# Holding the issue order of three engines in the last down units of a macaron decoder trunk, and handing finished tiles of x on one per product

## The chip, the cores and the metric

The kernel runs on one core of a Trainium2 chip. The metric is device time in microseconds (us). The engines are named as the profile names them: PE (TensorE, matmuls), DVE (VectorE), ACT (ScalarE), POOL (GpSimd) and SP (SyncE, which here only issues DMAs). Each engine runs its own list of instructions in order and waits for the others by semaphores.

## The reference

Two layers of a decoder work on x, 512 tokens by 1024 channels. Each layer is a half-weighted feed-forward block, a mixer, and another half-weighted feed-forward block, all with an RMS norm in front:

```python
def swiglu(x, w_gate, w_up, w_down):
    return (jax.nn.silu(x @ w_gate) * (x @ w_up)) @ w_down

for layer in range(DEPTH):                  # DEPTH = 2, D_MODEL = 1024, D_FF = 2816
    x = x + 0.5 * swiglu(rms_norm(x, ffn1_norm[layer]), ...)
    hn = rms_norm(x, mix_norm[layer])
    x = x + (pool_mla_mixer(hn, ...) if layer % 2 == 0 else gated_conv_mixer(hn, ...))
    x = x + 0.5 * swiglu(rms_norm(x, ffn2_norm[layer]), ...)
```

So there are four feed-forward blocks: the first ends into the attention mixer, the second into the third, the third into the convolution mixer, and the fourth into the stores of the output.

## The kernel before

x lies transposed in SBUF as eight tiles `x[0]` to `x[7]` of 128 channels by 512 tokens. All matrix products are done in split precision: each operand is a high part (`hi`, fp32r) and a low part (`lo`, the rest), and `mm3` or `product` (L489) issues three matmuls for each block, `hi*hi`, `hi*lo`, `lo*hi`. Weights come from memory in fp32. The function `split` makes the two parts: ACT casts (`whi`, L87), then DVE subtracts (`wlo`, L88). Three pairs of `whi`/`wlo` buffers go round, so a split can start only when the product three places earlier has left its buffer.

A feed-forward block is cut into units: `gate_up` units, one for each pair of hidden blocks, and `down` units, which add two by two tiles into x. Each unit is a block matrix product done in seven smaller products, P1 to P7, instead of eight (Strassen's scheme in Winograd's form). The sums of weight blocks that this needs are made by DMA: after P1, P5 and P6 have split their weight tile (`ar` or `sto`), a POOL-issued DMA adds the next block into the same tile (`Seven.add`, L124), and a later product of the unit (P7, P6, P3) splits that sum. The sums of activation blocks are made on DVE (`blocks`), and `put` splits them into `hh` tiles (L87 and L88 again).

A fixed list, made by `staggered`, says in which order the products of all units come. Its last part, with unit 12 the last `gate_up` and 13 and 14 the last two `down` units, is

```
12.P6 12.P2 12.P7 12.P3 12.P4  13.P1 13.P5 13.P2 13.P6 14.P5 13.P7 14.P1 13.P3 13.P4  14.P6 14.P2 14.P7 14.P3 14.P4
```

This text calls it the tail; there are four of them. A product is named by unit and step. One of unit 12 has 24 matmuls of 128x256, one of units 13 and 14 has 18 (three hidden blocks). `weights()` is called at the start of each product and emits the split for the product two places later. The result of a down product is added into two tiles of x (`add`, L560). Tiles 0 and 1 are final after 13.P3, 2 and 3 after 13.P4, 4 and 5 after 14.P3, 6 and 7 after 14.P4.

A final tile is handed to the next stage by `after(k)`. In the first three blocks that is `norm_in`: ACT squares it (`sq`, L247), POOL adds the square to `acc` (L252, L254), ACT scales it into the high part `xs` (L241) and DVE makes the low part (L242). For `k == 4` it also runs a small square root `d` (L260), which makes ACT load the table for square roots. In the last block `after` is `store`, a DMA to the output. Before the change all four tiles of a down unit are handed on after its P4.

The order on each engine isn't the order of the text: a scheduler places every instruction by its own estimate of when it can run, within the dependencies. Only the program order of what is emitted, plus that estimate, decides what stands ahead of what.

Of the kernel before, what the change touches and what calls it, by code (L numbers as in the profile page):

```python
# [1 line left out]

# [1 line left out]

# [32 lines left out]
GROUPS = ((0, 4), (4, 8), (8, 11))  # L37
# [4 lines left out]
def trunk(ctx: ExitStack, tc: tile.TileContext, a, out):  # L42
# [12 lines left out]
    nc = tc.nc  # L55
# [8 lines left out]
    def bank(tag="bank", bufs=None):  # L64
        return pp.tile([P, 512], F32, tag=tag, name=tag, bufs=bufs)
# [82 lines left out]
    def staggered(kinds, full):  # L148

        order = [(0, "P5"), (0, "P1")]
        for i, kind in enumerate(kinds):
            if i == full + 1:
                order += [(i, s) for s in ("P1", "P5", "P2", "P6")]
                order += [(i + 1, "P5"), (i, "P7"), (i + 1, "P1"), (i, "P3"), (i, "P4")]
            else:
                order += [(i, s) for s in ("P6", "P2", "P7")]
                if i + 1 == len(kinds) or i == full:
                    order += [(i, "P3"), (i, "P4")]  # L160
                else:
                    order += [(i + 1, "P5"), (i, "P3"), (i + 1, "P1"), (i, "P4")]
        return order
# [3 lines left out]
    for l in range(2):  # L167
        for f in ("ffn1", "ffn2"):
# [15 lines left out]
            what = []  # L184
            for gi, (p0, p1) in enumerate(GROUPS):
                last = gi + 1 == len(GROUPS)
# [3 lines left out]
            for kind, p in what:  # L190
                if kind == "gu":
                    units.append(seven([gu[p, q] for q in range(4)], CH, turn))
                else:
                    gi, e = p
                    p0, p1 = GROUPS[gi]
                    n = 2 * (p1 - p0) * P
                    w = a[f"{f}_w_down{gi}"][l]
                    units.append(seven([w[e, q] for q in range(4)], n, turn))
            order = staggered([k for k, _ in what], max(j for j, (k, _) in enumerate(what) if k == "gu"))
# [2 lines left out]
    ready = []  # L202
    loaded = [0]
    used = [0]

    def weights(ahead=3, fetched=6):
        i = used[0]
        used[0] += 1
        while len(ready) < min(i + ahead, len(chunks)):
            while (loaded[0] < min(max(len(ready) + 1, i + fetched), len(chunks))  # L210
                   and chunks[loaded[0]].turn <= now[0]):
                chunks[loaded[0]].load()
                loaded[0] += 1
            ready.append(chunks[len(ready)].halves())
        return ready[i]
# [124 lines left out]
    def ffn(l, f, which, after, first=False):  # L340
        what, order = plans[l, f]
        with ExitStack() as es:
# [139 lines left out]
            def product(ps, e, w, acts, fresh):  # L482
                hi, lo = w
                for k, (ah, al) in enumerate(acts):
                    s = slice((e * len(acts) + k) * P, (e * len(acts) + k + 1) * P)
                    o = ps[:, e * HT:(e + 1) * HT]
                    last = e == 1 and k == len(acts) - 1
                    for i, (w_, a_) in enumerate(((hi, ah), (hi, al), (lo, ah))):
                        nc.tensor.matmul(o, w_[:, s], a_, start=fresh and e == 0 and k == 0 and i == 0,  # L489
                                         stop=last and i == 2, skip_group_check=True)  # L490
# [54 lines left out]
            def down(i, p, s):  # L545
                gi, e0 = p
                p0, p1 = GROUPS[gi]
                u = live.setdefault(i, {})
                if s in ("P1", "P5", "P2"):
                    u[{"P1": "X", "P5": "Y", "P2": "Z"}[s]] = bank()  # L550
                ps = u["Z" if s == "P2" else "Y" if s in ("P5", "P3") else "X"]
                w = weights()
                for e in range(2):
                    product(ps, e, w, [hfac[q][right[s]] for q in range(p0, p1)], s in ("P1", "P5", "P2"))
                o11, o12, o21, o22 = (xt[:, 4 * e0 + 2 * i2:4 * e0 + 2 * i2 + 2, j * HT:(j + 1) * HT]
                                      for i2 in range(2) for j in range(2))
                v = ps.rearrange("p (e t) -> p e t", t=HT)

                def add(o, sign):
                    nc.vector.scalar_tensor_tensor(o, v, 0.5 * sign, o, ALU.mult, ALU.add)  # L560

                add({"P1": o11, "P2": o11, "P6": o12, "P3": o12, "P7": o22, "P5": o22, "P4": o21}[s],
                    -1.0 if s in ("P7", "P3", "P4") else 1.0)
                if gi == len(GROUPS) - 1 and s == "P4":
                    for k in range(4 * e0, 4 * e0 + 4):
                        after(k)

            for n, (i, s) in enumerate(order):
                if n == 3:
                    blocks(1, hz, False)  # L570
                    blocks(1, hz, True)
                kind, p = what[i]
                (gate_up if kind == "gu" else down)(i, p, s)

    def store(m):
        (nc.sync if m % 2 else nc.scalar).dma_start(out=out[m], in_=x[m])
# [371 lines left out]
    def odd_mixer(after):  # L948
        with tc.tile_pool(name="op", bufs=1) as op:
# [31 lines left out]
            for m in range(NK):  # L981
# [3 lines left out]
                after(m)  # L985

    ffn(0, "ffn1", 0, lambda m: norm_in(m, 1), True)
    even_mixer(lambda m: norm_in(m, 2))
    ffn(0, "ffn2", 2, lambda m: norm_in(m, 3))
    ffn(1, "ffn1", 3, lambda m: norm_in(m, 4))  # L990
    odd_mixer(lambda m: norm_in(m, 5))
    ffn(1, "ffn2", 5, store)
# [71 lines left out]
```

## Time and profile before

| what | value |
|---|---|
| median of three runs | 1735.53 us (1734.84 to 1741.09) |
| the profiled execution, its own time | 1735.6 us |
| its span, first to last instruction | 1733.9 us |
| granted clock of PE, mean | 0.996 of full speed |
| PE busy | 1692.3 us, 98% |
| DVE busy | 1312.8 us, 76% |
| ACT busy | 889.7 us, 51% |
| POOL busy | 299.2 us, 17% |

The profile is of one execution. A span runs from the first to the last instruction, and 1.7 us of the execution's own time lie around it. Busy shares are means over all stages. A matmul's end is modelled, so a matmul of 128x256 is drawn 0.28 us long although the next may start 0.11 us after it: an idle time that the profile shows on PE is therefore about 0.16 us shorter than the time in which PE could have started another.

### The profile page before, as it was taken

To read this page: it belongs to the slowest core of one execution; us is meant where nothing else is said; L and a number is where in the kernel's file an instruction comes from. 1 tells how busy PE (TensorE), PEld (TensorE's weight loads), DVE (VectorE), ACT (ScalarE), POOL (GpSimd) and SP (SyncE) were. 2 spreads that over 40 slices of the span, in tenths; PEclk is the share of its full clock that TensorE was granted. 3 is DMA by queue.
4 is the path that set the end of the run, shared out by engine and by line. 5 is a ranking of instruction groups with operands and counts; after the bars stand their busy time and mean duration, and the time that the engine had idled before them with its cause. 6 is when DMAs were issued, how large, how long until landed. Compare 5 with 4: busy or idle time off the path is not lost.

```text
span 1733.9 us, 30670 instructions
## 1 busy us (share of the span) xinstructions
PE 1692.3 (98%) x12354; PEld 1574.8 (91%) x12354; DVE 1312.8 (76%) x1883; ACT 889.7 (51%) x1268; POOL 299.2 (17%) x343
## 2 busy tenths in 40 slices
PE   7999999999999999999999999999999999999998
PEld 5799999977888899999988999998888879999998
DVE  5977786877897977786798867868655678867766
ACT  5554554564665564554565545545322345545553
POOL 2021111234202012111221112112000201121111
PEclk8999999999999999999999999999999999999999
DMA  6489988741015489989756898896322247998985
GB/s 219 108 213 221 220 213 213 160 147 37 19 43 169 119 217 215 217 219 217 158 179 148 218 223 205 212 208 138 112 98 98 97 142 180 211 218 210 216 209 131
DMA packets 86878, 294.76 MB, mean 170 GB/s; under 512 B 10448, under 2 KB 11216, under 8 KB 86736
## 3 DMA queue, kind: packets, MB, share of 16 engines
q0 software_dynamic: 34560, 121.65, 39.9%
q1 hardware_dynamic: 50512, 169.89, 28.0%
q8 instruction: 97, 1.59, 0.4%
q10 hardware_dynamic: 1664, 1.26, 0.2%
q14 instruction: 45, 0.37, 0.1%
HBM read 290.67 MB, written 2.10 MB: 169 GB/s over the span
## 4 chain that ended last, share of the span: by engine, by line
PE 82%; DVE 9%; issue 4%; ACT 2%; DMA 2%; POOL 1%; SPq 0%; ACTq 0%; DVEq 0%; POOLq 0%
PE bank L489 59%; PE bank L220 6%; PE bank L218 6%; PE bank L219 6%; DVE wlo L88 2%; DMA sto<-in_ffn_w_down 1%; ACT whi L87 1%; DVE xn L379 1%; DMA sto<-in_ffn_w_gu 1%; PE bank L895 1%; DVE xs L242 1%; PE held L218 0%; PE held L219 0%; PE held L220 0%; DVE x L560 0%
## 5 line engine op out<-in xcount | busy, mean ns | idle before, releaser
L489 PE MATMUL bank<-hh,whi 128*128 128x256 f32 x2464 | 427.6, 277 | 6.5 <-ACT whi L87 3.6
L489 PEld LDWEIGHTS bank<-hh,whi 128*128 128x128 f32 x2464 | 373.0, 188 | 9.8 <-ACT whi L87 4.6
L489 PE MATMUL bank<-hh,wlo 128*128 128x256 f32 x1232 | 340.5, 277 | 5.4 <-DVE wlo L88 5.4
L87 ACT CAST whi<-sto 128x1024 fp32r<-128x1024 f32 (+1 forms) x180 | 183.5, 1021 | 242.6 <-PE bank L489 140.0
L489 PE MATMUL bank<-fT,whi 128*128 128x256 f32 x1728 | 303.6, 278 | 0.0
L88 DVE TENSOR_TENSOR wlo<-sto,whi 128x1024 fp32r<-128x1024 f32 (+1 forms) x180 | 214.1, 1189 | 97.0 <-ACT whi L87 96.1
L489 PEld LDWEIGHTS bank<-fT,whi 128*128 128x128 f32 x1728 | 262.2, 188 | 2.0 <-ACT x L495 1.5
L489 PE MATMUL bank<-fT,wlo 128*128 128x256 f32 x864 | 239.1, 278 | 0.0
L489 PEld LDWEIGHTS bank<-hh,wlo 128*128 128x128 f32 x1232 | 231.1, 188 | 6.2 <-DVE wlo L88 6.2
L489 PE MATMUL bank<-fN,whi 128*128 128x256 f32 x1152 | 208.3, 283 | 3.5 <-ACT x L495 0.7
L218 PE MATMUL bank<-xs,whi 128*128 128x512 f32 x520 | 206.0, 397 | 2.5 <-DVE t L456 2.0
L220 PE MATMUL bank<-xs,wlo 128*128 128x512 f32 x520 | 204.4, 394 | 3.2 <-DVE wlo L88 3.1
L219 PE MATMUL bank<-xs,whi 128*128 128x512 f32 x520 | 204.9, 394 | 1.8 <-DVE xs L242 1.5
L489 PE MATMUL bank<-fB,whi 128*128 128x256 f32 x1152 | 205.9, 278 | 0.0
L87 ACT CAST whi<-a 128x1024 fp32r<-128x1024 f32 (+1 forms) x120 | 123.0, 1025 | 139.1 <-PE bank L489 88.0
L124 POOL DMA_DIRECT2D sto<-in_ffn_w_gu x108 | 94.4, 874 | 565.6 <-DVE wlo L88 285.3
L489 PEld LDWEIGHTS bank<-fN,whi 128*128 128x128 f32 x1152 | 174.2, 188 | 13.8 <-DVE c L532 8.4
L88 DVE TENSOR_TENSOR wlo<-a,whi 128x1024 fp32r<-128x1024 f32 (+1 forms) x120 | 142.6, 1188 | 53.0 <-ACT whi L87 52.7
L88 DVE TENSOR_TENSOR wlo<-ar,whi 128x1024 fp32r<-128x1024 f32 (+1 forms) x120 | 142.5, 1188 | 49.2 <-ACT whi L87 49.0
L87 ACT CAST whi<-ar 128x1024 fp32r<-128x1024 f32 (+1 forms) x120 | 122.6, 1021 | 106.1 <-PE bank L489 59.2
L489 PEld LDWEIGHTS bank<-fB,whi 128*128 128x128 f32 x1152 | 176.3, 188 | 0.0
L87 ACT CAST whi<-raw 128x1024 fp32r<-128x1024 f32 (+2 forms) x91 | 86.9, 958 | 163.6 <-PE bank L219 143.1
(242 smaller groups left out, 3028.9 us busy)
## 6 DMA issues: line engine op xcount, KB each, us to landing
sto<-in_ffn_w_gu POOLq DMA_DIRECT2D x108, 512.0 KB, 7.5
a<-in_ffn_w_gu SPq DMA_DIRECT2D x72, 512.0 KB, 6.2
sto<-in_ffn_w_down POOLq DMA_DIRECT2D x48, 512.0 KB, 7.7
sto<-in_ffn_w_gu SPq DMA_DIRECT2D x36, 512.0 KB, 4.7
ar<-in_ffn_w_gu SPq DMA_DIRECT2D x36, 512.0 KB, 5.4
ar<-in_ffn_w_gu POOLq DMA_DIRECT2D x36, 512.0 KB, 5.5
a<-in_ffn_w_down SPq DMA_DIRECT2D x32, 512.0 KB, 6.2
raw<-in_ffn_w_gu SPq DMA_DIRECT2D x31, 512.0 KB, 4.6
```

The costliest lines, as they stand in the source:

```text
L87: nc.scalar.copy(hi, raw)
L88: nc.vector.tensor_sub(lo, raw, hi.bitcast(F32))
L124: nc.gpsimd.dma_start(out=self.unit[tag], in_=self.srcs[q], accum_op=ALU.add)
L218: nc.tensor.matmul(ps, wh, ah, start=start, stop=False)
L219: nc.tensor.matmul(ps, wh, al, start=False, stop=False)
L220: nc.tensor.matmul(ps, wl, ah, start=False, stop=stop)
L242: nc.vector.scalar_tensor_tensor(xl, x[k], g, xh.bitcast(F32), ALU.mult, ALU.subtract)
L379: nc.vector.scalar_tensor_tensor(xn[e][:, i], x[k], gains[:, which, k:k + 1], R if e else Rp, ALU.mult, ALU.mult)
L489: nc.tensor.matmul(o, w_[:, s], a_, start=fresh and e == 0 and k == 0 and i == 0, stop=last and i == 2, skip_group_check=True)
L895: nc.tensor.transpose(ps[:, kt * P:(kt + 1) * P], p[:, kt * P:(kt + 1) * P], ident)
```

## The change

From 12.P6 on to the end of each feed-forward block, a context manager gives every instruction of PE, DVE and ACT a dependency, without a semaphore, on the instruction of the same engine that was emitted before it. The scheduler then keeps these three engines in program order there. POOL, SP and the DMAs aren't held. And tiles of x are handed on earlier and singly: 0 and 1 become available at 13.P3, 2 and 3 at 13.P4, and one is handed on at the end of each down product from there on, so tile 0 after 13.P3, 1 after 13.P4, 2 after 14.P6, 3 after 14.P2, none after 14.P7, 4 after 14.P3, 5 after 14.P4, and 6 and 7 right behind.

```diff
+    @contextmanager
+    def in_order():
+
+        traced = nc.cur_bb.bb.instructions
+        n = len(traced)
+        yield
+        before = {}
+        for k, i in enumerate(traced):
+            if i.engine in (nc.tensor.engine, nc.vector.engine, nc.scalar.engine):
+                if k >= n and i.engine in before:
+                    tc.add_manual_dep(i, before[i.engine], mybir.DependencyInfo(
+                        mybir.DependencyClass.NoSync, mybir.DependencyReason.DATA), reason="in_order")
+                before[i.engine] = i.name
...
-                if gi == len(GROUPS) - 1 and s == "P4":
-                    for k in range(4 * e0, 4 * e0 + 4):
-                        after(k)
-
+                if gi == len(GROUPS) - 1 and s in ("P3", "P4"):
+                    k = 4 * e0 + 2 * (s == "P4")
+                    done.extend((k, k + 1))
+                if done:
+                    after(done.pop(0))
+
+            done = []
+            last = order.index((len(what) - 3, "P6"))
+            pin = ExitStack()
             for n, (i, s) in enumerate(order):
+                if n == last:
+                    pin.enter_context(in_order())
                 if n == 3:
                     blocks(1, hz, False)
                     blocks(1, hz, True)
                 kind, p = what[i]
                 (gate_up if kind == "gu" else down)(i, p, s)
+            for k in done:
+                after(k)
+            pin.close()
```

Lines behind the new function stand 14 higher in the changed kernel (L560 becomes L574, L242 becomes L256), and L87 and L88 keep their numbers.

The first place is DVE in the first tail, from the result `c` of 12.P3 on. `hz` are activation blocks that are rebuilt, `hh` their low parts, and `wlo<-sto` is the split for 13.P5, `wlo<-a_3518` that for 13.P2. Before:

```order
L536 SCALAR_TENSOR_TENSOR c<-bank,x_3479 128x512
L88 TENSOR_TENSOR wlo<-sto,whi 128x768
L502 TENSOR_TENSOR hz<-c 128x256
L438 TENSOR_TENSOR hz<-hz 128x256
L440 SCALAR_TENSOR_TENSOR hz<-hz 128x256
L439 TENSOR_TENSOR hz<-hz 128x256
L542 SCALAR_TENSOR_TENSOR hz<-bank,c 128x256
L88 TENSOR_TENSOR hh<-hz,hh 128x512 x2
L88 TENSOR_TENSOR hh<-hz,hh 128x256
L448 SCALAR_TENSOR_TENSOR hz<-hz 128x256
L88 TENSOR_TENSOR wlo<-a_3518,whi 128x768
L88 TENSOR_TENSOR hh<-hz,hh 128x512
```

In the changed kernel the same stretch of DVE reads:

```order
L550 SCALAR_TENSOR_TENSOR c<-bank,x_3479 128x512
L516 TENSOR_TENSOR hz<-c 128x256
L452 TENSOR_TENSOR hz<-hz 128x256
L453 TENSOR_TENSOR hz<-hz 128x256
L454 SCALAR_TENSOR_TENSOR hz<-hz 128x256
L88 TENSOR_TENSOR hh<-hz,hh 128x512 x2
L88 TENSOR_TENSOR hh<-hz,hh 128x256
L88 TENSOR_TENSOR wlo<-sto,whi 128x768
L556 SCALAR_TENSOR_TENSOR hz<-bank,c 128x256
L462 SCALAR_TENSOR_TENSOR hz<-hz 128x256
L88 TENSOR_TENSOR hh<-hz,hh 128x512
L88 TENSOR_TENSOR wlo<-a_3518,whi 128x768
```

The split for 13.P5 moved from the second place to behind the three low parts of the rebuilt blocks, and the split for 13.P2 moved behind the last of them. On ACT the cast for 13.P5 likewise moved from ahead of the three `hh` casts to behind them.

The second place is DVE later in the same tail, from the add of 13.P3 on: `x<-bank` is the add of a down product, `xs` the low part of a tile handed on, and `wlo` the splits for 14.P2, 14.P7, 14.P3 and 14.P4. Before:

```order
L560 SCALAR_TENSOR_TENSOR x<-bank,x 128x2x256
L88 TENSOR_TENSOR wlo<-a_3762,whi 128x768
L242 SCALAR_TENSOR_TENSOR xs_3864<-x,gains,xs_3864 128x512
L560 SCALAR_TENSOR_TENSOR x<-bank,x 128x2x256
L242 SCALAR_TENSOR_TENSOR xs_3864<-x,gains,xs_3864 128x512
L88 TENSOR_TENSOR wlo<-ar,whi 128x768
L560 SCALAR_TENSOR_TENSOR x<-bank,x 128x2x256
L242 SCALAR_TENSOR_TENSOR xs_3875<-x,gains,xs_3875 128x512 x2
L560 SCALAR_TENSOR_TENSOR x<-bank,x 128x2x256
L88 TENSOR_TENSOR wlo<-sto,whi 128x768
L88 TENSOR_TENSOR wlo<-a_3835,whi 128x768
```

In the changed kernel the same stretch reads:

```order
L574 SCALAR_TENSOR_TENSOR x<-bank,x 128x2x256
L256 SCALAR_TENSOR_TENSOR xs_3839<-x,gains,xs_3839 128x512
L88 TENSOR_TENSOR wlo<-a_3762,whi 128x768
L574 SCALAR_TENSOR_TENSOR x<-bank,x 128x2x256
L256 SCALAR_TENSOR_TENSOR xs_3839<-x,gains,xs_3839 128x512
L88 TENSOR_TENSOR wlo<-ar,whi 128x768
L574 SCALAR_TENSOR_TENSOR x<-bank,x 128x2x256
L256 SCALAR_TENSOR_TENSOR xs_3900<-x,gains,xs_3900 128x512
L88 TENSOR_TENSOR wlo<-sto,whi 128x768
L574 SCALAR_TENSOR_TENSOR x<-bank,x 128x2x256
L256 SCALAR_TENSOR_TENSOR xs_3900<-x,gains,xs_3900 128x512
L88 TENSOR_TENSOR wlo<-a_3842,whi 128x768
```

Add, low part and split now follow each other in every product; the two low parts that stood together ahead of the split for 14.P3 (`wlo<-sto`) are parted, and every split stands behind the low part of the product before.

The third place is ACT at the very start of the program, which the change doesn't name: the five small square roots `d` were all placed there before, since they depend on a constant alone. Before:

```order
L260 ACTIVATE d<-eps 128x1 x5
L87 CAST whi<-raw 128x2x256
L241 ACTIVATE xs_122<-x,gains 128x512
L247 ACTIVATE sq<-x 128x512
L241 ACTIVATE xs_122<-x,gains 128x512
L87 CAST whi<-raw 128x2x256
L247 ACTIVATE sq<-x 128x512
L241 ACTIVATE xs_129<-x,gains 128x512 x2
L241 ACTIVATE xs_151<-x,gains 128x512
L247 ACTIVATE sq<-x 128x512 x2
```

In the changed kernel ACT starts with:

```order
L87 CAST whi<-raw 128x2x256
L255 ACTIVATE xs_122<-x,gains 128x512 x2
L87 CAST whi<-raw 128x2x256
L255 ACTIVATE xs_129<-x,gains 128x512 x2
L261 ACTIVATE sq<-x 128x512 x2
L255 ACTIVATE xs_151<-x,gains 128x512
L261 ACTIVATE sq<-x 128x512 x2
L255 ACTIVATE xs_151<-x,gains 128x512
```

The square roots left for the tails, and the first square now comes behind the fourth scaled tile instead of behind the first. Elsewhere, outside the tails and the first matmuls behind them, the lists of DVE and ACT are the same.

## Rows read from the trace of the kernel before

**Rows 1.** The first line of the page: span and instructions.

```profile
span 1733.9 us, 30670 instructions
```

**Rows 2.** Waits of PE: who waited for whom; us in total, times, longest.

```profile
PE held L316 <- DVE acc L322: 6.8, 1, 6.8
PE bank L489 <- DVE wlo L88: 6.3, 6, 1.7
PE bank L489 <- ACT whi L87: 3.6, 5, 0.8
...
PE bank L489 <- DVE hh L88: 1.8, 4, 0.5
...
PE bank L219 <- DVE xs L242: 1.5, 4, 0.6
...
PE bank L489 <- ACT hh L87: 1.0, 4, 0.3
```

**Rows 3.** Timeline of PE, first tail: start, length, [idle before <- releaser].

```profile
319.20 0.50 PE L489 MATMUL bank<-hh,whi 128*128 128x256 f32 x2 [0.85 <-ACT whi L87]
...
353.36 0.38 PE L489 MATMUL bank<-hh,wlo 128*128 128x256 f32 x1 [1.58 <-DVE wlo L88]
353.58 0.40 PE L489 MATMUL bank<-hh,whi 128*128 128x256 f32 x2
...
357.34 0.39 PE L218 MATMUL bank<-xs,whi 128*128 128x512 f32 x1
```

**Rows 4.** Timeline of ACT, first tail: casts for 13.P5, rebuilt blocks, 13.P3.

```profile
323.92 0.84 ACT L87 CAST whi<-sto 128x768 fp32r<-128x768 f32 x1 [2.73 <-PE bank L489]
...
326.57 1.59 ACT L87 CAST hh<-hz 128x512 fp32r<-128x512 f32 x3
...
337.97 0.83 ACT L87 CAST whi<-sto 128x768 fp32r<-128x768 f32 x1 [2.32 <-DMA sto<-in_ffn_w_down]
```

**Rows 5.** Timeline of POOL, first tail: accumulating DMAs after 13.P5, 13.P6; adds of squares.

```profile
326.15 0.86 POOL L124 DMA_DIRECT2D sto<-in_ffn_w_down  x1 [4.74 <-DVE hz L502]
333.14 0.88 POOL L124 DMA_DIRECT2D sto<-in_ffn_w_down  x1 [6.13 <-DVE wlo L88]
...
347.59 3.70 POOL L254 TENSOR_TENSOR acc<-acc,sq 128x512 f32<-128x512 f32 x2 [0.57 <-ACT sq L247]
```

**Rows 6.** Timeline of DVE, first tail.

```profile
324.00 0.69 DVE L536 SCALAR_TENSOR_TENSOR c<-bank,x 128x512 f32<-128x512 f32 x1 [2.35 <-PE bank L489]
324.79 0.96 DVE L88 TENSOR_TENSOR wlo<-sto,whi 128x768 fp32r<-128x768 f32 x1
...
333.26 0.95 DVE L88 TENSOR_TENSOR wlo<-sto,whi 128x768 fp32r<-128x768 f32 x1
...
334.72 0.95 DVE L88 TENSOR_TENSOR wlo<-ar,whi 128x768 fp32r<-128x768 f32 x1
...
345.09 0.75 DVE L242 SCALAR_TENSOR_TENSOR xs<-x,gains,xs 128x512 fp32r<-128x512 f32 x1 [0.29 <-ACT xs L241]
...
346.36 1.21 DVE L242 SCALAR_TENSOR_TENSOR xs<-x,gains,xs 128x512 fp32r<-128x512 f32 x1
...
348.96 2.87 DVE L242 SCALAR_TENSOR_TENSOR xs<-x,gains,xs 128x512 fp32r<-128x512 f32 x2
```

**Rows 7.** Timeline of PE, last tail: a late split.

```profile
1724.80 0.38 PE L489 MATMUL bank<-hh,wlo 128*128 128x256 f32 x1 [0.49 <-DVE wlo L88]
```

**Rows 8.** Timeline of ACT and of POOL, start of the program.

```profile
5.47 0.61 ACT L247 ACTIVATE sq<-x 128x512 f32<-128x512 f32 x1
...
8.97 2.05 ACT L241 ACTIVATE xs<-x,gains 128x512 fp32r<-128x512 f32 x3
...
11.68 6.70 POOL L254 TENSOR_TENSOR acc<-acc,sq 128x512 f32<-128x512 f32 x4 [1.18 <-ACT sq L247]
```

**Rows 9.** Timeline of POOL and ACT, last tail: accumulating DMA after 14.P5, then 14.P6's cast.

```profile
1707.01 0.88 POOL L124 DMA_DIRECT2D sto<-in_ffn_w_down  x1 [0.60 <-DVE wlo L88]
...
1714.80 0.84 ACT L87 CAST whi<-sto 128x768 fp32r<-128x768 f32 x1 [2.46 <-DMA sto<-in_ffn_w_down]
```

More of the change, by code (lines that the diff above doesn't have):

```diff
@@ L1 @@
-from contextlib import ExitStack
+from contextlib import ExitStack, contextmanager
 import numpy as np
```

## The prediction

> **What bounds the kernel now.** I read the page first, then PE's waits, then the tails in the timelines of all engines. The page's span is 1733.9 us [rows 1], and PE is busy for 98% of it, so only what PE waits for can be won, and every new wait of PE is lost time. The reader should see in the list of PE's waits [rows 2] how little there is. One wait of 6.8 us is at the start of the program (the sums for the first norm). The other five lines come to 6.3 + 3.6 + 1.8 + 1.5 + 1.0 = 14.2 us. The timeline of the first tail shows where these come from [rows 3]: 0.85 us at 319.20, where the scheduler had put two matmuls of 13.P1 ahead of 12.P4 and their weights weren't cast yet; waits for the rebuilt `hh` blocks in 13.P1 (the two `hh` lines, 2.8 us over four tails); and 1.58 us at 353.36, where DVE made two low parts of x (2.87 us, row 348.96 of [rows 6]) ahead of the split for 14.P3. So the whole stock is 14.2 us by the rows, some 3 us more by the 0.16 us that a matmul's drawn end hides at each of about 20 waits, and 0.5% of the time is 8.7 us, about what a measurement of this kernel can tell from no change. To be faster by that, the change would have to empty half of the stock without a new wait.
>
> The pace: from 353.58 to 357.34 PE issued 33 matmuls [rows 3], 0.114 us each. A product of unit 12 (24) takes 2.73 us, one of units 13 and 14 (18) takes 2.05 us.
>
> **The change, part by part.** All times are for the first tail; the other two with a norm behind them are taken alike.
>
> *The order from 12.P7 to 13.P6.* The 0.85 us wait goes, since 12.P3 now follows 12.P7 at once. But splits move behind the rebuilding of blocks, and that chain decides. I follow it in absolute times. The last matmul of 12.P7 starts at 319.20 - 0.85 - 0.28 = 318.07. With 24 matmuls each, 12.P3's result is there at 318.07 + 2.73 + 0.28 = 321.1, and 12.P4 ends at 318.07 + 0.11 + 5.46 = 323.65. On DVE the split for 13.P1 now stands ahead of reading that result, so `c` starts at about 321.8 instead of 324.00 [rows 6], 2.2 us earlier. Before, the three `hh` casts ended at 326.57 + 1.59 = 328.16 [rows 4]; 2.2 us earlier, and up to 0.4 more because the split at 324.79 no longer stands between `c` and `hz`, gives about 325.6. 13.P1 waits for these blocks as before, about 0.9 us (2.8 / 4 by the rows, and some of the hidden 0.16s), and ends at 323.65 + 2.05 + 0.9 = 326.6.
> - 13.P5: its cast stood ahead of this chain, at 323.92 [rows 4]; now it stands behind the three casts. 325.6 + 0.84 for the cast + 0.96 for the low part [rows 4, 6] = 327.4. The product's third matmul, the first that needs the low part, would start at 326.6 + 0.23: it waits 0.6 us. 13.P5 ends at 326.6 + 2.05 + 0.6 = 329.25.
> - 13.P2: it needs the block rebuilt from 12.P4's result, whose two steps on DVE now come behind that split, and its own split comes last. From 327.4: two steps on 256 columns, estimated at half of the 0.69 that `c` takes for 512 [rows 6], an `hh` cast of 1.59 / 3 = 0.5, a cast of 0.84 and a low part of 0.96 make 330.4 to 330.6; the third matmul would start at 329.5. It waits 1.1 us, and 13.P2 ends at 332.4.
> - 13.P6: its weight tile is summed by a DMA that may start only when 13.P5's split has read the tile. Before, POOL issued it at 326.15 [rows 5], now at about 327.5. The same kind of DMA, issued at 333.14, let the cast start at 337.97 [rows 4, 5], 4.8 us later. So 332.3, a cast of 0.84 and a low part of 0.96 make 334.1; the third matmul would start at 332.6. It waits 1.5 us, and 13.P6 ends at 332.4 + 2.05 + 1.5 = 335.95.
>
> Before, 14.P3 started at 353.36 - 1.58 - 0.40 = 351.38 [rows 3] and eight products of 2.05 us without a long wait lie between, so 13.P6 ended at 335.0. The change makes it **later by 1.0 us**, the won 0.85 us counted. Bounds: +0.5 if each of the three chains is 0.15 us shorter, and with a slower DMA as under the rivals.
>
> *The tiles handed on one per product.* No operation is added or removed, each tile has its square, POOL add, scaled cast and low part as before. Before, PE lost 1.58 + 0.16 = 1.74 us. Now DVE has, per product, a split and an add, 334.72 - 333.26 = 1.46 us [rows 6], and one low part. That took 0.75 us beside POOL's short copy, 1.21 us for the second tile, and 2.87 / 2 = 1.43 us for the third and fourth, while POOL added squares (3.70 us for two, [rows 5]). A square, its POOL add and the low part belong to one tile, so the new order does not part them: the low part follows the square by the length of one cast. I take 1.2 to 1.4 us for tiles 1 to 3. Then DVE needs 2.7 to 2.9 us per product against PE's 2.05, over by 0.6 to 0.8 in three products running, 1.8 to 2.4 us in all. Splits have a lead, but ACT too now stands between: cast, square and scaled cast follow one another, and a cast waits for them. I leave 0.6 us for the lead: PE loses about 1.4 us. **Net -0.3 us.** Bounds: -1.7 (0.75 us for each tile; 2.2 against 2.05 is covered by the lead), +0.7 (1.43 us and no lead).
>
> The Trainium skill (SBUF — State Buffer, section "SBUF: two separate sides") says that a DVE instruction with two inputs in SBUF and a GpSimd instruction that reads SBUF exclude each other for a whole instruction, whoever starts first. By that rule spacing the tiles out wins nothing on these low parts, and the sum is the one above; without it, it would be that of the first rival. The trace agrees with the rule so far as the low part's 0.75 us becomes 1.21 to 1.43 us while POOL adds.
>
> *The end of the tail.* Tiles 4 and 5 start earlier. But DVE now takes the add of 14.P4 behind a second split for the next stage, which waits in ACT's list for tile 4's square and scaled cast, which wait for the add of 14.P3. So tiles 5 to 7 come no earlier. Before, PE lost some 0.3 us per tail there (1.5 us in 4 waits, one at the start of the program [rows 2]). I take **+0.3 us**, bounds 0 and +1.0. The table load and `d` in ACT's list lie in the time in which ACT waits for the add of 14.P3, so they cost nothing; without that cover the load, not shown in these rows, would sit ahead of tile 4's square, which is inside the +1.0.
>
> *The last tail.* Stores need no ACT or DVE work, so only the first part counts there: +1.0, less the wait of 0.49 + 0.16 us for a split [rows 7], which came up among four stores issued at once: **+0.4 us**.
>
> *The start of the program.* The first square starts behind the fourth scaled cast, at about 8.97 + 1.2 = 10.2 less the 0.5 us of the square that no longer stands ahead = 9.7, instead of 5.47 [rows 8]. POOL's five adds could start when the second square is done, 9.7 + 0.6 + 0.5 = 10.8 and the copy of the first behind it, so about 11.0. At 6.70 / 4 = 1.68 us each they end at 19.4 at the latest, against 11.68 + 6.70 = 18.4, and earlier if they meet less of DVE. PE waits for their sum (6.8 us, [rows 2]): **+0.7 us**, bounds +0.3 and +1.1.
>
> **The sum.** Three tails at 1.0 - 0.3 + 0.3 = +1.0, the last +0.4, the start +0.7: +4.1 us. The profiled execution took 1735.6 us, its span and 1.7 us around it, which is also the median of the runs (1735.53). So **1739.7 us**, 0.24% more: no change that a measurement tells.
>
> **The rivals.**
> 1. *The spread tiles are cheap.* Each low part takes 0.75 us, the chain to 13.P6 comes out at its lower bound, nothing is lost at the end of the tail: 3 x (0.5 - 1.7) + (0.5 - 0.65) + 0.3 = -3.5 us, 1732.1 us. For it: POOL's adds, spaced out, collide less with each other's neighbours. Against it: the pairing within one tile.
> 2. *The summing DMA becomes the bound, and it is slower.* Each microsecond of a later landing of the sum for 13.P6 comes straight onto PE, in four tails, since no slack is left there. In the last tail a DMA of this kind took from 1707.01 to 1714.80, 7.8 us [rows 9], with another one ahead of it. 3.0 us more than 4.8 in each tail gives +12 us, 1751.7 us: slower. It decides from 1.2 us more on (4.1 + 4 x 1.2 = 8.9 us). Against it: for 13.P6 the queue is empty ahead of the DMA, and the row of 4.8 us is from such a place.
> 3. *The waits of the tails simply go.* Program order is the order in which PE needs things, the new waits are smaller than I think: up to -14.2 + 0.7 us, 1722 us. Against it: the chain above, in which every split stands behind work for a later product.
>
> **How the numbers follow.** The forecast has 0.48, rival 1 0.28, rival 2 0.17, rival 3 0.07. Faster by over 0.5% needs rival 3: 0.07. Slower by over 0.5% (above 1744.2 us) is rival 2; all upper bounds at once would get there too, which I count with it: 0.17. The rest, 0.76, is within 0.5%. The range reaches down past rival 1 to 1731 and up to 1747, which takes in the upper bounds of the unknown costs together (3 x (1.0 + 0.7 + 1.0) + 0.4 + 1.1 = 9.6 us, 1745.2) and rival 2 up to a landing 1.8 us later.
>
> **What the profile after would show.** The 0.85 us wait ahead of 13.P1 gone; new waits on `wlo` at the third matmul of 13.P5, 13.P2 and 13.P6, the last behind a cast that waits for a DMA; waits of 0.4 to 0.8 us on `wlo` in 14.P7 to 14.P4 instead of one of 1.58; low parts of 1.2 us and more next to POOL's adds; the first norm's wait of PE at 7.5 us. The prediction is wrong if 13.P5 and 13.P2 start without a wait, or if the splits of unit 14 keep pace.

## The result and the profile after

The changed kernel takes 1749.16 us (median of 4 runs, 1748.21 to 1750.17) against 1736.61 us for the kernel before beside it: 1.0072 times as long, 95% interval 1.0056 to 1.0089. It is slower by 0.72%, 12.5 us. The forecast was 1739.7 us in a range of 1731 to 1747: wrong, and wrong on the side to which I gave 0.17.

The page of the profile after begins with this span [rows 1]:

```profile
span 1746.4 us, 30669 instructions
```

The list of PE's waits (us in total, times, longest) answers to [rows 2]:

```profile
PE held L330 <- DVE acc L336: 7.7, 1, 7.7
PE bank L503 <- DVE x L574: 6.9, 5, 2.0
PE bank L503 <- DVE c L546: 6.3, 5, 1.5
PE bank L503 <- DVE wlo L88: 6.3, 14, 0.6
PE bank L503 <- ACT whi L87: 3.3, 4, 0.9
```

The second and the third line have no counterpart before: in them PE waits for a bank that DVE has still to read, for an add to x (L574) or for `c` of 12.P7 (L546). PE's timeline of the first tail shows the places [rows 3]:

```profile
320.65 0.50 PE L503 MATMUL bank<-fN,whi 128*128 128x256 f32 x2 [1.46 <-DVE c L546]
...
329.35 0.38 PE L503 MATMUL bank<-hh,wlo 128*128 128x256 f32 x1 [0.33 <-DVE wlo L88]
...
332.52 0.38 PE L503 MATMUL bank<-hh,wlo 128*128 128x256 f32 x1 [0.49 <-DVE wlo L88]
...
335.49 0.51 PE L503 MATMUL bank<-hh,whi 128*128 128x256 f32 x2 [0.81 <-ACT whi L87]
...
336.48 0.38 PE L503 MATMUL bank<-hh,wlo 128*128 128x256 f32 x1 [0.49 <-DVE wlo L88]
...
354.88 0.48 PE L503 MATMUL bank<-hh,whi 128*128 128x256 f32 x2 [2.02 <-DVE x L574]
...
360.14 0.50 PE L503 MATMUL bank<-hh,whi 128*128 128x256 f32 x2 [0.40 <-DVE x L574]
```

These are, in order, the first matmul of 12.P3, the third of 13.P5, the third of 13.P2, the first and third of 13.P6, the first of 14.P7 and the first of 14.P4. DVE's timeline says why the first and the sixth are late [rows 6]:

```profile
319.90 0.69 DVE L546 TENSOR_TENSOR c<-bank,x 128x512 f32<-128x512 f32 x1
...
348.78 0.75 DVE L256 SCALAR_TENSOR_TENSOR xs<-x,gains,xs 128x512 fp32r<-128x512 f32 x1 [1.31 <-ACT xs L255]
...
350.98 1.19 DVE L256 SCALAR_TENSOR_TENSOR xs<-x,gains,xs 128x512 fp32r<-128x512 f32 x1
352.10 2.03 DVE L88 TENSOR_TENSOR wlo<-ar,whi 128x768 fp32r<-128x768 f32 x1
354.05 0.68 DVE L574 SCALAR_TENSOR_TENSOR x<-bank,x 128x512 f32<-128x512 f32 x1
354.65 0.74 DVE L256 SCALAR_TENSOR_TENSOR xs<-x,gains,xs 128x512 fp32r<-128x512 f32 x1
355.32 2.04 DVE L88 TENSOR_TENSOR wlo<-sto,whi 128x768 fp32r<-128x768 f32 x1
```

12.P3 goes on in the bank of 12.P5, from which DVE reads for the `c` of 12.P7; that step ends at 320.59, and PE goes on at 320.65. 14.P7 goes on in the bank of 14.P6. The add that reads this bank comes at 354.05, since it stands behind a tile's low part and a split of 2.03 us; the same split takes 0.96 us elsewhere. POOL's timeline has an add of squares beside each of the two long splits, and the issue of 13.P6's summing DMA [rows 5]:

```profile
329.70 0.86 POOL L124 DMA_DIRECT2D sto<-in_ffn_w_down  x1 [5.67 <-DVE hz L556]
...
352.02 1.30 POOL L268 TENSOR_TENSOR acc<-acc,sq 128x512 f32<-128x512 f32 x1 [0.39 <-ACT sq L261]
354.77 1.78 POOL L268 TENSOR_TENSOR acc<-acc,sq 128x512 f32<-128x512 f32 x1 [1.45 <-ACT sq L261]
```

ACT casts that weight tile and the next one from here on [rows 4]:

```profile
334.60 1.56 ACT L87 CAST whi<-sto 128x768 fp32r<-128x768 f32 x2 [3.13 <-PE bank L503]
```

The row names PE as the releaser, but the sum landed 4.8 us after its issue at 329.70, just ahead of the cast.

In the last tail 13.P6 waits as in the first, and the wait of [rows 7] is gone (PE's timeline):

```profile
1717.70 0.50 PE L503 MATMUL bank<-hh,whi 128*128 128x256 f32 x2 [0.87 <-ACT whi L87]
...
1718.69 0.38 PE L503 MATMUL bank<-hh,wlo 128*128 128x256 f32 x1 [0.49 <-DVE wlo L88]
```

At the start POOL's adds end at 19.6 us, against 18.4 in [rows 8] (POOL's timeline):

```profile
11.76 7.83 POOL L268 TENSOR_TENSOR acc<-acc,sq 128x512 f32<-128x512 f32 x5
```

**Where the time went.** Both traces hold 12354 matmuls, so the n-th of one can be set against the n-th of the other. At the end of 12.P7 in the first tail the changed kernel is 0.8 us behind. From there to the end of 13.P6 it falls back by 2.85, 2.85, 2.95 and 2.91 us in the four tails: 11.6 us. Between there and the next tail, what the tiles and the next stage's start do included, it falls back by 1.1, 1.8 and 0.6 us; the end of the last tail wins 0.9. 2.4 us come off between the second and the third tail, where the kernel before issued its matmuls 0.118 us apart for a while and the changed one 0.113, both at a granted clock of 1.00; why, no run shows.

### The profile page after: what moved, and what is told of

It reads as the page before. It is cut to its first block, busy times and chain, and to the rows that moved or that the text cites. A ratio compares the mean times of both kernels' runs of the same rounds, so it can differ in the third digit from the quotient of the medians.

```text
span 1746.4 us, 30669 instructions
## 1 busy us (share of the span) xinstructions
PE 1692.1 (97%) x12354; PEld 1573.9 (90%) x12354; DVE 1313.8 (75%) x1883; ACT 889.7 (51%) x1269; POOL 296.9 (17%) x343
## 4 chain that ended last, share of the span: by engine, by line
PE 81%; DVE 11%; ACT 3%; issue 3%; DMA 2%; POOL 1%; SPq 0%; ACTq 0%; DVEq 0%; POOLq 0%
PE bank L503 58%; PE bank L234 6%; PE bank L232 6%; PE bank L233 6%; DVE wlo L88 3%; ACT whi L87 1%; DMA sto<-in_ffn_w_gu 1%; DVE xn L393 1%; PE bank L919 1%; DVE c L546 0%; DVE fT L88 0%; PE held L232 0%; PE held L233 0%; DVE fB L88 0%; POOL acc L268 0%
## 5 line engine op out<-in xcount | busy, mean ns | idle before, releaser
L87 ACT CAST whi<-sto 128x1024 fp32r<-128x1024 f32 (+1 forms) x180 | 183.5, 1021 | 233.7 <-PE bank L503 129.5
L88 DVE TENSOR_TENSOR wlo<-sto,whi 128x1024 fp32r<-128x1024 f32 (+1 forms) x180 | 216.3, 1202 | 101.3 <-ACT whi L87 100.7
L87 ACT CAST whi<-a 128x1024 fp32r<-128x1024 f32 (+1 forms) x120 | 122.8, 1023 | 133.0 <-PE bank L503 80.1
L88 DVE TENSOR_TENSOR wlo<-a,whi 128x1024 fp32r<-128x1024 f32 (+1 forms) x120 | 142.6, 1188 | 54.7 <-ACT whi L87 54.6
L88 DVE TENSOR_TENSOR wlo<-ar,whi 128x1024 fp32r<-128x1024 f32 (+1 forms) x120 | 145.8, 1215 | 47.7 <-ACT whi L87 47.2
L87 ACT CAST whi<-ar 128x1024 fp32r<-128x1024 f32 (+1 forms) x120 | 122.4, 1020 | 99.4 <-PE bank L503 60.3
L87 ACT CAST whi<-raw 128x1024 fp32r<-128x1024 f32 (+2 forms) x91 | 86.9, 957 | 155.5 <-PE bank L233 135.1
```

The source lines that it names most:

```text
L87: nc.scalar.copy(hi, raw)
L88: nc.vector.tensor_sub(lo, raw, hi.bitcast(F32))
```

## The experiments

Two theories stood at the start. A: the held order from 12.P7 to 13.P6 costs nearly everything. B: the tiles handed on one per product do. The table gives times as ratios to the kernel before, measured beside each run; 0.1% is 1.7 us, and single runs of one kernel spread by some 4 us to either side. Diffs are against the changed kernel unless the text says otherwise.

| run | ratio | 95% interval |
|---|---|---|
| the change | 1.0072 | 1.0056 to 1.0089 |
| pin_only | 1.0165 | 1.0143 to 1.0186 |
| tiles_only | 1.0010 | 0.9998 to 1.0022 |
| fresh_bank | 1.0045 | 1.0029 to 1.0062 |
| short_adds | 1.0029 | 1.0017 to 1.0041 |
| pin_pe | 1.0046 | 1.0030 to 1.0062 |
| pin_dve_act | 1.0061 | 1.0049 to 1.0073 |
| split_ahead | 1.0036 | 1.0024 to 1.0049 |
| own_bank | 1.0020 | 1.0008 to 1.0033 |
| one_later | 1.0088 | 1.0068 to 1.0109 |
| later_tiles | 1.0005 | 0.9994 to 1.0016 |
| own_split_pin | 1.0022 | 1.0011 to 1.0033 |
| three_undone | 0.9974 | 0.9965 to 0.9983 |
| before_short | 0.9959 | 0.9947 to 0.9972 |
| late_squares | 1.0037 | 1.0024 to 1.0051 |
| dve_adds | 0.9972 | 0.9959 to 0.9986 |
| dve_adds_start | 0.9968 | 0.9956 to 0.9980 |

**pin_only and tiles_only: one half of the change each.**

```diff
-                if gi == len(GROUPS) - 1 and s in ("P3", "P4"):
...
-                if done:
+                if gi == len(GROUPS) - 1 and s == "P4":
+                    done.extend(range(4 * e0, 4 * e0 + 4))
+                while done:
                     after(done.pop(0))
```

> Program order held from 12.P6 on, but the four tiles of x handed on together behind 13.P4 and behind 14.P4, as in the kernel before. Theory A (the order from 12.P7 to 13.P6 costs about 3.0 us in each of four tails, and the tiles little): the 12 us of the four tails stay, and four low parts in a row on DVE, held ahead of the add of 14.P6, make PE wait 3 to 4 us there in three tails, so 1748 to 1752 us, no better than the changed kernel. Theory B (the tiles handed on one per product cost most of the 12.5 us): most of it goes, 1737 to 1741 us.

```diff
-                if n == last:
-                    pin.enter_context(in_order())
```

> Only the tiles handed on one per product; the order is left to the scheduler. It moves the split for 14.P3 ahead of the fourth tile's low part and the add of 14.P6 ahead of the third's, so Theory A: the wait of 1.58 us ahead of 14.P3 falls to 0.3 us or less, and three tails win 1.2 to 1.7 us each: 1731 to 1733 us. Theory B: the splits run into POOL's adds here too (2.0 us instead of 0.96), the adds of x come late, and the time is 1738 us or more.

Theory B falls: the tiles alone change nothing, the held order alone costs 1.65%, about twice what I gave it. PE's timeline of pin_only shows the wait that I had named:

```profile
358.60 0.76 PE L503 MATMUL bank<-hh,whi 128*128 128x256 f32 x2 [3.82 <-DVE x L574]
```

Its windows show what I had not (us; busy time and instructions of PE, PEld, DVE, ACT and POOL; granted clock; share and GB/s of the DMA engines):

```profile
352.00:355.00 3.00, 2.78 (x24) 2.57 (x22) 3.00 (x3) 2.56 (x5) 2.84 (x3) 1.00 0.72 212
358.00:361.00 3.00, 2.40 (x11) 2.43 (x12) 2.79 (x4) 0.00 (x0) 0.50 (x2) 0.50 0.04 1
361.00:364.00 3.00, 3.00 (x16) 3.00 (x15) 1.02 (x3) 1.04 (x1) 0.00 (x0) 0.50 0.49 144
```

After the wait of 3.82 us the granted clock stands at 0.50 (1.2 GHz), with 16 matmuls in 3 us where 24 ran at 1.00; such a wait comes in three tails. So the tiles one per product are worth 0.9% in a held order and nothing in a free one. In tiles_only the wait of 1.58 us in 14.P3 went, but 0.99 us came ahead of 14.P4, which goes on in the bank of 14.P7: DVE reads that bank only from 353.22 to 353.90, and PE goes on at 354.04. My 0.2 to 0.3% gain there did not come.

**fresh_bank and short_adds: one resource each, with the same order on every engine.** In fresh_bank 12.P3 opens a bank:

```diff
+                own = s == "P3" and i == len(what) - 3
+                if own:
+                    u["Y"] = bank()
```

> The changed kernel, with 12.P3 accumulating in a bank of its own, so that it need not wait until DVE has read 12.P5's and 12.P3's bank for the result of 12.P7; the order on every engine stays as it is. The product of 12.P5 is left out of the second sum by this. Theory A1 (12.P3's wait for the bank shifts the whole chain behind it): the wait of 1.46 us goes, 13.P1 waits some 0.5 us more for its blocks, the waits of 13.P5, 13.P2 and 13.P6 keep their sizes, and each of four tails wins 1.2 to 1.6 us: 1743 to 1744.5 us. Theory A2 (the splits' chain on ACT and DVE ends last whatever PE does): the later waits grow by what 12.P3 wins, 1748 to 1750 us.

In short_adds the tails call `squares(k, 16)`, so POOL adds 16 of 512 columns:

```diff
-            nc.gpsimd.tensor_add(Norm.acc, Norm.acc, sq)
+            nc.gpsimd.tensor_add(Norm.acc[:, :n], Norm.acc[:, :n], sq[:, :n])
```

> The changed kernel, with POOL's adds of squares cut from 512 columns to 16 in the tails (the start of the program keeps them); most squares are left out of the norm by this, and the order on every engine stays. Theory C1 (DVE's low parts take 2.0 us instead of 0.95 because POOL's add is under way, and that makes the adds of x late): the low parts of the weights ahead of 14.P6's and 14.P2's adds take 0.96 us again, the wait of 2.02 us ahead of 14.P7 falls to 0.6 us or less and that of 0.40 ahead of 14.P4 goes, three tails win 1.5 to 2.2 us each: 1742.5 to 1744.7 us. Theory C2 (the held order alone, with a tile's low part ahead of the split and the add, makes them late): the wait stays above 1.3 us, 1747 to 1749 us.

Both win: 0.27% and 0.43%. In fresh_bank, 0.9 us above the range of A1 and 2.6 below that of A2, the wait of 1.46 us is gone, and what stands behind keeps its size (PE's timeline):

```profile
326.35 0.39 PE L503 MATMUL bank<-hh,whi 128*128 128x256 f32 x1 [0.36 <-DVE hh L88]
...
328.44 0.38 PE L503 MATMUL bank<-hh,wlo 128*128 128x256 f32 x1 [0.34 <-DVE wlo L88]
...
331.62 0.38 PE L503 MATMUL bank<-hh,wlo 128*128 128x256 f32 x1 [0.49 <-DVE wlo L88]
...
334.48 0.51 PE L503 MATMUL bank<-hh,whi 128*128 128x256 f32 x2 [0.72 <-ACT whi L87]
```

So A1 holds in the trace: the bank's wait shifts the whole chain. In short_adds the split takes 0.95 us again and 14.P7 waits 0.49 (DVE's and PE's timelines):

```profile
352.29 0.95 DVE L88 TENSOR_TENSOR wlo<-ar,whi 128x768 fp32r<-128x768 f32 x1
```

```profile
353.99 0.47 PE L503 MATMUL bank<-hh,whi 128*128 128x256 f32 x2 [0.49 <-DVE x L574]
```

**pin_pe and pin_dve_act: which engine's order.** The edit is the tuple of engines in `in_order`.

> The changed kernel with program order held on TensorE alone; VectorE and ScalarE are left to the scheduler. Theory A3 (what costs in the tails is that splits are held behind the rebuilding of blocks and behind the tiles, so VectorE's and ScalarE's order): 12.P3 still waits 1.46 us for its bank, but 13.P5, 13.P2 and 13.P6 wait for hardly anything and the add of 14.P6 comes in time, so a loss of no more than 0.5 to 1 us in each of four tails: 1737 to 1741 us. Theory A4 (TensorE's own held order, above all 12.P3 straight behind 12.P7, is the cost): 1745 us or more.

> The changed kernel with program order held on VectorE and ScalarE and TensorE left to the scheduler. Theory A3: the waits of 13.P5, 13.P2, 13.P6 (3.6 us in each tail with what the drawn ends hide) and the 2.0 us ahead of 14.P7 stay, 1745 to 1750 us. Theory A4: most of the loss goes, 1737 to 1741 us.

A3 holds for the second only: with TensorE free and the other two held, 12.P4 follows 12.P7 and waits 0.73 us for a copy, but the waits of 13.P5, 13.P2 and 13.P6 stay (0.34, 0.49, 0.88 and 0.49 us), and so does the time. With TensorE alone held I was wrong: DVE's free list has the split for 13.P1 ahead of `c`, and 12.P3's wait grows (PE's timeline):

```profile
319.65 0.50 PE L503 MATMUL bank<-fN,whi 128*128 128x256 f32 x2 [2.44 <-DVE c L546]
```

With this wait the granted clock fell to 0.50 in three of the four tails. Either hold costs more than half of the whole, so their costs do not add up: one bad place is exchanged for another.

**split_ahead, own_bank, own_split_pin: repairing the tail.**

```diff
                     gated(c, hz[:, B12])
+                    if i == len(what) - 3:
+                        early.append(weights())
                     blocks(p, hz, False)
```

> The changed kernel with one row moved on ScalarE and one on VectorE in each tail: cast and low part of 13.P5's weights stand ahead of the rebuilding of 12.P3's blocks, not behind it. If the held place of this split is what makes 13.P5 and, by the summing DMA that may start only behind it, 13.P6 wait: 13.P5's 0.33 us goes, the DMA for 13.P6 is issued some 2.5 us sooner and the 0.8 us wait on its cast goes, 13.P1 waits up to 1 us longer for its blocks; 1 to 1.6 us won in each of four tails, 1743 to 1745.5 us. If not (the blocks' delay costs what the split wins): 1747.5 to 1750 us.

0.36% is won, as the first theory there said: 13.P5's wait and that on 13.P6's cast are gone, 13.P2's 0.49 us stays, and 13.P1 waits 0.59 and 0.36 us for its blocks. The subtraction for own_bank stands behind 12.P7, and 12.P3 takes a bank as in fresh_bank:

```diff
                     gated(c, hz[:, N22], -1.0)
+                    if i == len(what) - 3:
+                        nc.vector.tensor_sub(u["x2"], u["x2"], u["Y"])
```

> The kernel before (nothing held, tiles as before), with 12.P3 accumulating in a bank of its own; the product of 12.P5, which it shared a bank with, is subtracted beforehand from the copy of 12.P6's result, one more step of 512 columns on VectorE in each tail, so the output is complete. If the bank that 12.P7's result still has to be read from is what the tail waits for before 13.P1: 12.P3 can follow 12.P7 at once, the wait of 0.85 us goes and the blocks are rebuilt about 2 us sooner, 1.2 to 1.8 us won in each of four tails, 0.3 to 0.4% faster than before. If the rebuilding is bound elsewhere: within 0.1% of before.

There is no gain in the free order. PE's timeline shows the wait come back at 13.P1, for the blocks:

```profile
329.77 0.38 PE L489 MATMUL bank<-hh,whi 128*128 128x256 f32 x1 [1.87 <-ACT hh L87]
```

The median is 0.20% above the kernel before, but the profiled execution is the fastest of its twelve (1735.51 us, mean granted clock 0.996) and loses nothing. In the other eleven the mean granted clock was 0.990 to 0.993; none of them was profiled, so what they lost stays open.

> The changed kernel with both repairs of the tail at once: 12.P3 in a bank of its own (with the subtraction on VectorE, so the output is complete) and 13.P5's split ahead of the rebuilding of blocks. If the two losses are separate: 3.8 us and 4.5 us are won, 1740 to 1742 us. If both end in the same chain (the blocks of 12.P3, which 13.P1 needs): 13.P1 waits 1.5 to 2.5 us for them and little more than one repair is won, 1743.5 to 1746 us. In neither case does it beat the kernel before, since the tiles still cost 1.2 us in each of three tails.

In the held order both repairs together win 0.50% of the 0.72%. Apart they won 0.27% and 0.36%, 0.63% in sum, which the intervals can't tell from 0.50%. 13.P1 waits 1.28 us for an `hh` cast.

**one_later and later_tiles: the tiles' places.** In one_later `after(done.pop(0))` stands ahead of `done.extend`.

> The changed kernel with every tile of x handed on one product later. In the changed kernel VectorE stands still 1.31 us at the first tile, whose scaled cast isn't ready, with a split and an add behind it. If that start is what makes the add of 14.P6 late: one tile fewer lies ahead of it, the wait of 2.02 us ahead of 14.P7 falls to 0.8 us or less, and three tails win 1 us or more each, less what the later tiles cost at the end of the tail: 1743 to 1747 us. If VectorE's load alone decides (2.9 us of work per product against 2.05 while POOL adds): the wait goes to the products behind, within 1 us of 1749.

> The kernel before (nothing held), with the tiles handed on later and apart: 0 and 1 behind 13.P4, 2 behind 14.P2, 3 behind 14.P7, 4 to 7 behind 14.P4 as before. The scheduler puts a split ahead of each of the later tiles' low parts. If the wait of 1.58 us ahead of 14.P3 is VectorE's order there alone: it goes, and three tails win 1 to 1.8 us, 0.2 to 0.3% faster than before. If VectorE's load in this stretch decides, as in the run with the tiles handed on one per product and nothing held: the wait comes back at 14.P4 or at the start of the next stage, within 0.1% of before.

Neither wins, and one_later comes out above both its theories. In its first tail the wait of 2.02 us is parted into 0.17 and 0.49 us in 14.P3 and 1.25 us ahead of 14.P4; in later_tiles 0.98 us comes ahead of 14.P4 in place of 1.58 in 14.P3. Every order tried moves the wait; taking load off DVE removes it (short_adds, before_short).

**three_undone, before_short, late_squares: whose price POOL's adds are.**

> The changed kernel, its held order kept, with the three causes taken away together: 12.P3 in a bank of its own, 13.P5's split ahead of the rebuilding of blocks, POOL's adds of squares cut to 16 columns in the tails (most squares are left out of the norm by this). If these three make up the 12.5 us and don't overlap: 7.2 us for the first two (measured together) and 6.8 us for the third, 1733.5 to 1737 us, the level of the kernel before. If something else in the held order costs too, or the shares overlap: 1738.5 us or more.

> The kernel before with POOL's adds of squares cut to 16 columns in the tails (most squares are left out of the norm by this), order on every engine as before. If DVE's meeting with POOL's adds is paid in the kernel before too: the two low parts of 2.87 us ahead of the split for 14.P3 fall to 1.5 us, the wait of 1.58 us there goes, three tails win 1.2 to 1.7 us each, 0.2 to 0.3% faster. If the held order alone makes it dear: within 0.1% of before.

The first theory of before_short holds, with more won than the 0.2 to 0.3% that I gave it, and it corrects what short_adds seemed to say. Cutting the adds wins 0.41% in the kernel before, 0.43% in the changed one and 0.48% in the repaired one. So DVE meeting POOL is paid in every order; it is no price of the change. DVE's timeline of before_short, against 2.87 us in [rows 6]:

```profile
348.76 1.49 DVE L242 SCALAR_TENSOR_TENSOR xs<-x,gains,xs 128x512 fp32r<-128x512 f32 x2
```

three_undone is 0.26% faster than before, which neither of its theories named, and 0.15% behind before_short, with intervals that overlap: nothing shows that the held order pays even when repaired. In late_squares (diff against own_split_pin) the meeting only moves:

```diff
+        if k < 4:
+            scaled(k, which)
+            return
         if k == 4:
+            for j in range(4):
+                squares(j)
```

> The changed kernel with the two repairs of the tail and with the squares of tiles 0 to 3 taken behind 14.P3's product, so that POOL's adds start some 8 us later and all squares are in the norm; the output is complete. If the place of POOL's adds is what matters: the low parts of the weights ahead of 14.P6's and 14.P2's adds take 0.96 us, the wait ahead of 14.P7 falls from 1.8 to 0.6 us or less, and it comes out within 0.15% of the kernel before, or up to 0.1% faster. If the collisions only move to the products behind and to the start of the next stage (14.P4's add, the last low parts, the norm's sum): 0.15 to 0.3% slower than before, as without this edit.

The wait ahead of 14.P7 is gone, and the next stage starts late (PE's timeline):

```profile
362.10 0.50 PE L232 MATMUL bank<-xs,whi 128*128 128x512 f32 x1 [1.18 <-ACT xs L255]
...
363.45 0.50 PE L233 MATMUL bank<-xs,whi 128*128 128x512 f32 x1 [0.85 <-DVE xs L256]
```

**dve_adds and dve_adds_start: the adds off POOL.** Against the kernel before; the second does it in `begin` only.

```diff
-            nc.gpsimd.tensor_add(Norm.acc, Norm.acc, sq)
+            nc.vector.tensor_add(Norm.acc, Norm.acc, sq)
```

> The kernel before, with the adds of squares on VectorE instead of GpSimd, at the start of the program and in the tails; the output is complete, nothing is held. An add takes some 0.68 us on VectorE (as its two late adds do) against 1.3 to 1.9 us on GpSimd, which stretches VectorE's own work by 0.45 to 1.1 us meanwhile. If VectorE doing the adds itself costs it no more than the meeting did: the first norm's wait of 6.8 us falls by 2 to 4 us, and the tails keep or better their 1.6 us; 0.1 to 0.4% faster than before. If VectorE, which has hardly a gap in the last 13 us of a tail, pays the adds in full ahead of the split for 14.P3: the tails lose 1 us or more each, and the sum is within 0.1% of before or slower.

> As the run before, but with the adds on VectorE only at the start of the program; the tails stay as in the kernel before. The start's share alone: the first norm's wait falls from 6.8 to 3 to 5 us, 0.1 to 0.2% faster; or the low parts of the weights, behind the adds on VectorE, take PE's place in waiting, and it is within 0.1%.

Both beat both kernels, by 0.28% and 0.32% against before, with a complete output. All of it comes from the start: PE's wait of 6.8 us for the first norm's sum is gone, and 2.8 us for a cast take its place. That is 4.0 us; by the 200th matmul dve_adds_start is 5.8 us ahead. The granted clock has a part in the rest: from 14 to 30 us of the span it was 0.89, and 0.68 before. An add takes 0.68 us on DVE, against POOL's 1.68 [rows 8] (DVE's timeline and PE's waits of dve_adds_start):

```profile
10.67 0.68 DVE L254 TENSOR_TENSOR acc<-acc,sq 128x512 f32<-128x512 f32 x1
```

```profile
PE bank L218 <- ACT whi L87: 2.8, 1, 2.8
```

In the tails DVE has no room for the adds: in dve_adds 0.56 and 1.30 us of waits in the first tail stand in place of 1.58. The Trainium skill (GPSIMD Engine Reference, section "3.1 Elementwise — side-by-side cycle accounting") says that VectorE is about twice as fast for such adds; the trace has 2.5 times, or 1.9 times against POOL's shortest add above (1.30 us). The tails show that this wins only where VectorE has time.

## Why the prediction was wrong

**The step that failed** is "The 0.85 us wait goes, since 12.P3 now follows 12.P7 at once". It follows in PE's list, but not in time: it accumulates in a bank that DVE reads only after ACT's copy of 12.P7's result. I followed splits and blocks and left this reuse of a bank out. In the kernel before the scheduler had put twelve other matmuls in between, two of 13.P1, the first of which waited 0.85 us [rows 3], and ten of 12.P4. PE's timeline there has the first of these ten at 319.69 and 12.P3's first at 320.97, without a wait:

```profile
319.69 0.50 PE L489 MATMUL bank<-fT,whi 128*128 128x256 f32 x2
...
320.97 0.40 PE L489 MATMUL bank<-fN,whi 128*128 128x256 f32 x2
```

In the changed kernel the read costs 1.46 us by its row in each of four tails, and in fresh_bank, without it, 0.27% comes back. Set against the sum, the order from 12.P7 to 13.P6 cost 11.6 us in the four tails where I had 4.0, and the tiles with the ends of three tails 3.5 us where I had nothing.

**The new waits** I had nearly right. I set 0.6, 1.1 and 1.5 us for 13.P5, 13.P2 and 13.P6. From the starts of successive matmuls, less the pace of 0.114 us and with the wider first step behind each wait, they are 0.60, 1.12 and 1.86, and 12.P3's is 1.73 (a wait's row shows less, since a matmul's drawn end hides part of it). Against this, 13.P1 waits 0.37 us instead of my 0.9, since PE comes later. Together that is 5.67 us, where I had 4.1. The same account gives 2.66 us for this stretch before; by counting back from 14.P3 I had put 13.P6's end 0.3 us too late there. So it is +3.0 us a tail for my +1.0. That a split held behind the blocks causes the waits of 13.P5 and 13.P6 is shown by split_ahead.

**The tiles.** I set 1.4 us of loss on splits against 1.74 before. It came as 2.02 and 0.40 us on banks of late adds, some 1.2 us worse than before. The mis-sized term is DVE's work per product: 2.7 to 2.9 us in my sum, 3.67 and 3.23 in the trace (from 350.98 to 354.65 and to 357.88). I had stretched the tile's low part alone; the split beside POOL's add was stretched by 1.07 us. The rule that I cited from the Trainium skill (SBUF — State Buffer, section "SBUF: two separate sides"), that an instruction of DVE with two inputs in SBUF and one of GpSimd that reads SBUF exclude each other, holds for a split as well, and the trace agrees: 2.03 us beside an add, 0.95 in short_adds.

**The start** came out as I said, 0.6 us at 310 us of the span for my 0.7, with PE's wait at 7.7 us where I had named 7.5, but partly by luck. Behind this wait PE was 1.2 us later than before; by the 60th matmul it had made that up, at a granted clock of 0.79 from 14 to 30 us of the span where it was 0.68 before; and it lost 0.9 us again from 54 to 66 us, at 0.72 where it was 0.86. **The end of the tail** can't be told from the tiles by these rows; the last tail came out worse (+2.0 for +0.4), by the first step.

**The rivals.** The summing DMA was not slower: issued at 329.70, cast at 334.60, 4.9 us for my 4.8. The cheap tiles and the tail without waits did not come.

**What is left:** own_split_pin lies 0.22%, 3.8 us, above the kernel before. Set against that kernel's trace matmul by matmul, it falls back by 0.4 to 0.6 us in each tail from 12.P7 to 13.P6, and by 2.2 us from there to the end of 14.P4 in each of the first three. There PE waits for the add of 14.P6, and the clock falls in all three (PE's timeline, first tail; windows of the three tails):

```profile
351.70 0.51 PE L504 MATMUL bank<-hh,whi 128*128 128x256 f32 x2 [1.78 <-DVE x L582]
```

```profile
352.00:355.00 3.00, 3.00 (x16) 3.00 (x15) 3.00 (x4) 0.46 (x1) 1.05 (x3) 0.50 0.00 0
877.60:881.00 3.40, 3.40 (x17) 3.40 (x18) 3.40 (x5) 0.44 (x1) 0.52 (x1) 0.51 0.15 24
1215.60:1219.00 3.40, 3.40 (x18) 3.40 (x18) 3.40 (x6) 1.30 (x2) 0.00 (x0) 0.50 0.05 8
```

Its matmuls start 0.213 us apart there instead of 0.114, so 16 of them lose 1.6 us. In all its runs the mean granted clock was 0.990 to 0.993, and 0.992 to 0.996 in the kernel before beside it. That the clock is the whole of the 3.8 us is not shown: no run changes it alone.

## What to carry to other kernels

Before an order is held, list for each accumulating product who must still read its bank: a scheduler's odd interleaving may be the cover for just that read. Where a wait moves whenever the order is changed (tiles_only, later_tiles, own_bank, late_squares), stop reordering and take load off: moving five adds at the start from GpSimd to VectorE won 0.32%, where no order tried here beat the kernel before with a complete output.

## Not expected of the hardware

A short wait of PE can cost a second time. In the changed kernel PE waited 2.04 us in the second tail, up to 881.43; these are windows ahead of its end and behind it:

```profile
878.00:881.00 3.00, 1.39 (x13) 1.19 (x11) 3.00 (x3) 3.00 (x6) 2.03 (x3) 1.00 0.48 179
882.50:885.50 3.00, 3.00 (x16) 3.00 (x16) 3.00 (x5) 0.72 (x1) 0.00 (x0) 0.50 0.41 116
```

The granted clock was 0.50 (1.2 GHz) behind it and 1.00 (2.4 GHz) before. From 13.P6 to the end of 14.P4 this tail lost 1.9 us, the first and the third 1.2. In these two, waits of 2.02 and 2.03 us left the clock at 1.00, so it does not follow each time; in own_split_pin it followed three waits of 1.78 us.
